# A hybrid decoder block on one core: q, k and v projected channel-major and passed through DRAM

## The chip, the cores and the metric

One core of a Trainium2 chip. The core has four compute engines that run beside each other, each through its own instructions in order: TensorE (PE: matrix products and transposes), VectorE (DVE), ScalarE (ACT) and GpSimd (POOL). SyncE (SP) issues the transfers between DRAM and the on-chip memory (SBUF). Products land in PSUM, which POOL does not read here. The metric is the device time of one execution in microseconds (us); less is better.

## The reference, cut to what matters

All is float32; S = 2048 tokens, 1024 channels, 16 q heads and 4 k/v heads of 64 channels, blocks of 128 tokens.

```python
h = rmsnorm(x, norm_g)
proj = einsum("bsd,de->bse", h, w_in)        # 7680 columns
glu_in, conv_gate, q, k, v, attn_gate, merge_logits = split(proj)
a, b = split(glu_in); c = depthwise_causal_conv(a * sigmoid(b), 31 taps) + bias
c = silu(layernorm(c))
y_conv = (c * silu(conv_gate)) @ w_conv_out
q, k = rope(q), rope(k)      # halves t1, t2 of a head: t1*cos - t2*sin, t2*cos + t1*sin
# each block of 128 queries sees its own block and the one before, window 128, a sink per head
a = softmax_with_sink(q @ k.T / 8) @ v
y_attn = (a * silu(attn_gate)) @ w_attn_out
x = x + (sigmoid(m_c) * y_conv + sigmoid(m_a) * y_attn) @ w_out
return rmsnorm(x)
```

## The kernel before

The tokens go through in two sweeps of 1024, each of two halves of 512. A product in float32 is made as three products of two-part numbers: each operand is split into a rounded part (hi, a cast, mostly on ACT) and the rest (lo, a subtraction), and hi x hi, hi x lo and lo x hi are summed in PSUM.

`project` makes one item: 128 output channels (on partitions) over a sweep, that is 48 matmuls of 128x512, with weights loaded, cast and subtracted by `load_w`. The items of a sweep's first stage are the GLU (gb, ga: `glu_items`) and the gates ag, cg, ma, mc (`gate_item`, eight items each, written to DRAM as d_ag and so on). A GLU item starts one channel block of the convolution: 31 operations on DVE (`conv_ops`, L363 and L367) in a background queue (`line.bg`), issued one per `CONV_EVERY` of TensorE time.

Attention runs in 32 units per sweep (a k/v head g and a token block b: `unit_item`). A unit projects q, k and v of its 128 tokens token-major: 24 matmuls of 128x384 (tile qkv, L463) with weights wqh, wql of that head. Then `attention`, a chain of steps, goes: rope on DVE and POOL (ra, rb), splits into sq, transposes of q and k on TensorE (tq, tk), copies to qT and kT, scores (sc), softmax into ss, transposes of the probabilities (tpp), their split into pt, four selections on POOL that part current and earlier keys (pc, pt), the product with v (ov), and d_att to DRAM. After each step the chain waits for `LAT` us of emitted TensorE time.

```python
LAT = (10.0, 4.0, 15.0, 7.0)   # before tq, sc, tpp, ov
CONV_EVERY = 2.2
```

When all eight convolutions are done, the layer norm starts (`ln_chain`): sums split (csum), the mean by matmuls with ones (lnmu), then eight `ln_center`s on DVE with squares on ACT and the additions of vsum on DVE, then `ln_chain2`: the variance (lnvar), square root, four reciprocals, eight `ln_apply` (cv times rstd on DVE, silu on ACT).

The attention output is then gated: 16 `a_ops` per sweep, each of which loads a gate (lag) and an attention tile (latt) from DRAM through a pool of five buffers (t2k), multiplies them on DVE (L697) and splits the result (aT). `start_tail` releases 14 of them when attention is done and two more when the layer norm is. The items `ya` (attention projection, from aT), `yc` (convolution projection, from uT) and `out_item` follow. At the head of the first ya item stands `line.finish()`, which emits whatever is still waiting.

The order on TensorE is the order of the program text as `Line` emits it; the other engines' orders are set by a scheduler. Between units stand GLU items and gates; after the last unit `start_tail()` comes ahead of the gates that remain.

Of the kernel before, what the change touches and what calls it, by code (L numbers as in the profile page):

```python
# [16 lines left out]
ALU = mybir.AluOpType  # L17
# [18 lines left out]
QKV = GQ * HD + 2 * HD  # L36
# [13 lines left out]
def hybrid_block(ctx: ExitStack, tc: tile.TileContext, x, norm_g, w_in, conv_w, conv_b, ln_g, ln_b,  # L50
                 w_conv, sinks, w_attn, w_out, fin_g, cos_t, sin_t, out):
# [13 lines left out]
    win = w_in[0].rearrange("(k p) e -> p k e", p=P)  # L65
    wconv = w_conv[0].rearrange("(k p) e -> p k e", p=P)
    wattn = w_attn[0].rearrange("(k p) e -> p k e", p=P)
# [26 lines left out]
    def load_first(half):  # L94
        xs = []
        for j in range(4):
            r0 = (4 * half + j) * P
            xs.append(slot(A[8 + 4 * half + j], [P, D], F32, f"xf{half}_{j}"))
            nc.sync.dma_start(out=xs[-1], in_=x2[r0:r0 + P, :])
        return xs  # L100
# [4 lines left out]
    ident_r = const.tile([P, P], F32R, name="ident_r")  # L105
    ident = f(ident_r)
    ident_0 = slot(A[1], [P, P], F32, "ident_0")
    make_identity(nc, ident_0)
    dve.tensor_copy(out=ident_r, in_=ident_0)
    ones_0 = slot(A[2], [P, P], F32, "ones_0")  # L110
# [16 lines left out]
    NR = TAPS + 4  # L127
    rows = slot(A[0], [P, D], F32, "rows")
    nc.sync.dma_start(out=rows[0:TAPS], in_=conv_w[0])
    for i, r in enumerate((norm_g, conv_b, ln_g, ln_b)):  # L130
        nc.sync.dma_start(out=rows[TAPS + i:TAPS + i + 1], in_=r)
    par = const.tile([P, KC, NR], F32, name="par")
    tp = tp_ps.tile([P, 512], F32, tag="tp", name="tp_par")
    for k in range(KC):
        pe.transpose(out=tp[:, k * NR:(k + 1) * NR], in_=rows[0:NR, k * P:(k + 1) * P],
                     identity=ident[0:NR, 0:NR])
    dve.tensor_copy(out=par, in_=tp[:, 0:KC * NR].rearrange("p (k r) -> p k r", r=NR))
# [20 lines left out]
    d_kh = dram.tile([NKV, P, 2 * P], F32, name="d_kh")  # L158
    d_vh = dram.tile([NKV, P, 2 * HD], F32, name="d_vh")

# [1 line left out]
    class Line:  # L162
# [7 lines left out]
        def spend(self, us):  # L170
            """Tensor engine time was emitted: emit what falls due."""
# [3 lines left out]
            while True:  # L175
                if self.bg and self.bg_t <= self.t:
                    self.bg.popleft()()
                    self.bg_t += self.every
                    continue
                if not self.bg:  # L180
                    self.bg_t = max(self.bg_t, self.t)
                due = [c for c in self.late if c[0] <= self.t]
# [15 lines left out]
        def start(self, chain, ok=lambda: True):  # L198
            self.step(chain, ok)

# [30 lines left out]
    def load_w(src, name):  # L231
        """[1024, 128] columns of a matrix as its two float32r parts, by halves of the rows."""
# [11 lines left out]
    def project(src, rhs, name, evac):  # L244
        """128 output columns over the sweep's tokens, channels on partitions: an item for the line."""
# [5 lines left out]
        def blocks():  # L251
            for half in range(2):
# [11 lines left out]
        return prefetch, blocks  # L264
# [13 lines left out]
    def build_h(s, b, tiles):  # L278
        """x block b of sweep s: rmsnorm, transposed, split."""
# [35 lines left out]
    def build_h_first(half, xs):  # L315
        """As build_h, for four blocks at the start of the program."""
# [26 lines left out]
    def sweep(s):  # L343
# [13 lines left out]
        # -- gated linear unit and depthwise convolution --  # L357
# [25 lines left out]
        def glu_items(c):  # L383
# [15 lines left out]
            return [project(win[:, :, C_GLU_B + c * P:C_GLU_B + (c + 1) * P], h_rhs, f"gb{s}_{c}", ev_b),  # L399
                    project(win[:, :, C_GLU_A + c * P:C_GLU_A + (c + 1) * P], h_rhs, f"ga{s}_{c}", ev_a)]  # L400

        # -- gates, kept in DRAM until they are used --
        def gate_item(kind, col, func, e):
# [5 lines left out]
            return project(win[:, :, col + e * P:col + (e + 1) * P], h_rhs, f"{kind}{s}_{e}", ev)  # L409
# [6 lines left out]
        # -- attention --  # L416
        wq, kt, vt = {}, {}, {}

        def load_qkv(g):
            """The weights of a kv head's q, k and v, as eight pieces of work."""  # L420
            tiles, wq[g] = {}, []

            def load(k):
                kp, j = divmod(k, 2)
                if j == 0:
                    tiles["hi"] = slot(AT[2 * kp], [P, 2, QKV], F32R, f"wqh{s}_{g}_{kp}")
                    tiles["lo"] = slot(AT[2 * kp + 1], [P, 2, QKV], F32R, f"wql{s}_{g}_{kp}")
                hi, lo = tiles["hi"][:, j, :], tiles["lo"][:, j, :]
                if s == g == 0:
                    raw = slot(H[8 + k], [P, QKV], F32, f"rawq{s}_{g}_{k}")  # L430
                else:
                    raw = stage.tile([P, QKV], F32, tag="raw", name=f"rawq{s}_{g}_{k}")
                nc.sync.dma_start(out=raw[:, 0:GQ * HD],
                                  in_=win[:, k, C_Q + g * GQ * HD:C_Q + (g + 1) * GQ * HD])
                kv = win[:, k, C_K:C_K + 2 * NKV * HD].rearrange("p (a b) -> p a b", a=2)
                nc.sync.dma_start(out=raw[:, GQ * HD:QKV].rearrange("p (a b) -> p a b", a=2),
                                  in_=kv[:, :, g * HD:(g + 1) * HD])
                act.copy(hi, raw)
                split_lo(lo, raw, hi, pool)
                wq[g].append((hi, lo))  # L440

            return [lambda k=k: load(k) for k in range(KC)]

        done = {}

        def unit_item(g, b):
            got = {}

            def prefetch():
                blk = s * NB + b  # L450
                cs = work.tile([P, 2, HD], F32, tag="cs", name=f"cs{s}_{g}_{b}", bufs=2)
                nc.sync.dma_start(out=cs[:, 0, :], in_=cos_t[blk * P:(blk + 1) * P, :])
                nc.sync.dma_start(out=cs[:, 1, :], in_=sin_t[blk * P:(blk + 1) * P, :])
                got["cs"] = cs

            def blocks():
                ps = mm_ps.tile([P, TH], F32, tag="mm", name=f"qkv{s}_{g}_{b}")
                c0 = (b % 4) * P
                for k in range(KC):
                    hk = hT[b // 4][k]  # L460
                    whi, wlo = wq[g][k]
                    for i, (a, w) in enumerate(((hk[:, 0], whi), (hk[:, 0], wlo), (hk[:, 1], whi))):
                        pe.matmul(out=ps[:, 0:QKV], lhsT=a[:, c0:c0 + P], rhs=w,  # L463
                                  start=(k == 0 and i == 0), stop=(k == KC - 1 and i == 2))
                    if k == KC - 1:
                        n = g * NB + b
                        done[n] = 0
                        line.start(attention(g, b, got["cs"], ps),
                                   lambda: n == 0 or done[n - 1] > min(done[n] + 1, 4))
                    yield 3 * MM_US * QKV / TH  # L470

            return prefetch, blocks

        def attention(g, b, cs, ps):
            u = f"{s}_{g}_{b}"
            n = g * NB + b
            blk = s * NB + b
            cur = b % 2
            first = blk == 0
            nqk = GQ + 1  # L480
            pv = ps[:, 0:nqk * HD].rearrange("p (h d) -> p h d", d=HD)
            ra = t2k(f"ra{u}")[:, 0:nqk * HD].rearrange("p (h d) -> p h d", d=HD)
            rb = t2k(f"rb{u}")[:, 0:nqk * HD].rearrange("p (h d) -> p h d", d=HD)
            hh = HD // 2
            dve.tensor_tensor(out=ra, in0=pv, in1=cs[:, 0:1, :].broadcast_to([P, nqk, HD]), op=ALU.mult)
            pw = pv.rearrange("p h (a d) -> p h a d", d=hh)
            dve.tensor_tensor(out=rb.rearrange("p h (a d) -> p h a d", d=hh), in0=pw[:, :, ::-1, :],  # L487
                              in1=cs[:, 1:2, :].rearrange("p o (a d) -> p o a d", d=hh).broadcast_to(
                                  [P, nqk, 2, hh]), op=ALU.mult)
# [381 lines left out]
```

## Time and profile before

| | before |
|---|---|
| median of three runs | 2251.75 us (2247.3 to 2253.0) |
| span of the profiled execution | 2252.7 us |
| TensorE busy | 2111.2 us (94%) |
| VectorE busy | 1501.2 us (67%) |
| ScalarE busy | 970.0 us (43%) |
| GpSimd busy | 999.7 us (44%) |
| moved by DMA | 205.97 MB, 91 GB/s over the span |

The profile is of one execution, whose own time is its span of 2252.7 us; it lies 1 us above the median of the runs. Lines such as L463 are lines of the kernel file. The groups of instructions list `line engine operation out<-in shapes xcount | busy us, mean ns | idle before it, and what ended the idle time`.

### The profile page before, as it was taken

The page shows a single profiled execution, that of the slowest core. Times are in us where ns is not written, and L with a number is a line of the kernel's source. Part 1 is how long each engine was busy: PE and PEld are TensorE (multiplying, and loading weights), DVE is VectorE, ACT ScalarE, POOL GpSimd, SP SyncE. Part 2 cuts the span into 40 slices and gives each one's busy share as a digit, 9 for nine tenths or more (in the row PEclk, how much of TensorE's full clock was granted, in tenths as well). Part 3 has the DMA queues.
Part 4 walks back from the last instruction along what each step waited for, and adds up shares of the span by engine and source line. Part 5 has one row for each costly group of instructions (what it writes and reads, how often), then busy time and mean ns, then how long its engine had stood idle before and what let it go on. Part 6 is the DMA issues. An engine that isn't in the chain of part 4 may idle for free. (4 is left out here: it accounts for less than half of the span.)

```text
span 2252.7 us, 28431 instructions
## 1 busy us (share of the span) xinstructions
PE 2111.2 (94%) x10000; PEld 1760.6 (78%) x10000; DVE 1501.2 (67%) x2053; ACT 970.0 (43%) x2130; POOL 999.7 (44%) x771
## 2 busy tenths in 40 slices
PE   6998999899899998999999989998998999999998
PEld 6876887787788776888888778777877887878877
DVE  5788787978785746123658878879787858461224
ACT  6454435344535663123454453453444367531212
POOL 3466456446634421242044665565566544222400
PEclk9999999999999999999999999999999999999999
DMA  4122112211312256434331222122113122673331
GB/s 141 50 65 76 60 52 70 69 48 53 95 57 66 90 179 218 120 94 173 113 103 52 62 75 66 48 70 69 52 57 89 53 66 80 209 221 94 99 131 75
DMA packets 255862, 205.97 MB, mean 91 GB/s; under 512 B 48453, under 2 KB 207173, under 8 KB 255720
## 3 DMA queue, kind: packets, MB, share of 16 engines
q1 hardware_dynamic: 255720, 204.16, 29.3%
q8 instruction: 79, 1.29, 0.2%
q14 instruction: 63, 0.52, 0.1%
HBM read 152.98 MB, written 51.12 MB: 91 GB/s over the span
## 5 line engine op out<-in xcount | busy, mean ns | idle before, releaser
L367 DVE SCALAR_TENSOR_TENSOR cv<-glu,par,cv 128x1024 f32<-128x1024 f32 x480 | 730.4, 1522 | 9.3
L463 PE MATMUL qkv<-wqh,hT 128*128 128x384 f32 x1024 | 281.3, 338 | 0.0
L463 PEld LDWEIGHTS qkv<-wqh,hT 128*128 128x128 f32 x1024 | 188.2, 189 | 2.2
L816 PE MATMUL o<-wo,mT 128*128 128x512 f32 x768 | 183.2, 397 | 2.1 <-ACT wo L778 1.9
L559 POOL TENSOR_TENSOR ss<-ss,st 128x512 f32<-128x512 f32 x64 | 98.0, 1532 | 177.0 <-issue 55.2
L495 POOL TENSOR_TENSOR ra<-ra,rb 128x320 f32<-128x320 f32 x64 | 96.3, 1504 | 174.1 <-DVE rb L487 82.3
L463 PE MATMUL qkv<-wql,hT 128*128 128x384 f32 x512 | 172.9, 338 | 0.3 <-POOL wql L229 0.3
L816 PEld LDWEIGHTS o<-wo,mT 128*128 128x128 f32 x768 | 144.3, 189 | 35.0 <-ACT wo L778 2.3
L258 PE MATMUL mm_ya<-aT,whi_ya 128*128 128x512 f32 x512 | 161.7, 397 | 6.4 <-ACT whi_ya L239 3.2
L258 PE MATMUL mm_ag<-hT,whi_ag 128*128 128x512 f32 x512 | 164.1, 402 | 2.1 <-DVE hT L229 2.1
L258 PE MATMUL mm_gb<-hT,whi_gb 128*128 128x512 f32 x512 | 162.6, 399 | 0.9 <-DVE vn L229 0.9
L258 PE MATMUL mm_mc<-hT,whi_mc 128*128 128x512 f32 x512 | 159.9, 394 | 3.3 <-ACT whi_mc L239 3.3
L258 PE MATMUL mm_cg<-hT,whi_cg 128*128 128x512 f32 x512 | 163.0, 400 | 0.0
L258 PE MATMUL mm_ma<-hT,whi_ma 128*128 128x512 f32 x512 | 162.2, 398 | 0.0
L258 PE MATMUL mm_ga<-hT,whi_ga 128*128 128x512 f32 x512 | 159.0, 392 | 1.4 <-ACT glu L389 1.4
L258 PE MATMUL mm_yc<-uT,whi_yc 128*128 128x512 f32 x512 | 158.0, 390 | 0.0
L580 POOL TENSOR_SCALAR_AFFINE_SELECT pt<-pt 128x512 fp32r<-128x512 f32 x120 | 114.8, 956 | 91.7 <-DVE pt L229 85.7
L578 POOL TENSOR_SCALAR_AFFINE_SELECT pc<-pt 128x512 fp32r<-128x512 f32 x120 | 121.5, 1013 | 60.2 <-ACT pt L571 60.1
L555 ACT ACTIVATE ss<-ss,st 128x128 f32<-128x128 f32 x256 | 99.9, 391 | 60.8 <-DVE st L550 60.4
L258 PEld LDWEIGHTS mm_ya<-aT,whi_ya 128*128 128x128 f32 x512 | 97.2, 191 | 29.6 <-ACT whi_ya L239 5.0
L258 PEld LDWEIGHTS mm_mc<-hT,whi_mc 128*128 128x128 f32 x512 | 96.4, 189 | 24.3 <-ACT whi_mc L239 4.2
L258 PEld LDWEIGHTS mm_ag<-hT,whi_ag 128*128 128x128 f32 x512 | 97.2, 193 | 21.9 <-DVE hT L229 3.0
(176 smaller groups left out, 4666.0 us busy)
## 6 DMA issues: line engine op xcount, KB each, us to landing
rawq<-in_w_in_dram SPq DMA_DIRECT2D x64, 128.0 KB, 2.1
raw_gb<-in_w_in_dram SPq DMA_DIRECT2D x32, 256.0 KB, 3.1
raw_ga<-in_w_in_dram SPq DMA_DIRECT2D x32, 256.0 KB, 3.0
raw_ag<-in_w_in_dram SPq DMA_DIRECT2D x32, 256.0 KB, 3.1
d_att<-ss SPq DMA_DIRECT2D x64, 128.0 KB, 1.8
d_ag<-ag SPq DMA_DIRECT2D x32, 256.0 KB, 3.3
raw_cg<-in_w_in_dram SPq DMA_DIRECT2D x32, 256.0 KB, 3.1
d_cg<-cg SPq DMA_DIRECT2D x32, 256.0 KB, 3.4
```

The lines of the kernel that those rows point to most:

```text
L258: pe.matmul(out=ps, lhsT=a, rhs=b, start=(k == 0 and i == 0), stop=(k == KC - 1 and i == 2))
L367: dve.scalar_tensor_tensor(out=cv[c], in0=glu[c][:, j:j + T], scalar=tap(c, j), in1=cv[c], op0=ALU.mult, op1=ALU.add)
L463: pe.matmul(out=ps[:, 0:QKV], lhsT=a[:, c0:c0 + P], rhs=w, start=(k == 0 and i == 0), stop=(k == KC - 1 and i == 2))
L495: pool.tensor_tensor(out=ra, in0=ra, in1=rb, op=ALU.add)
L555: act.activation(out=sb[:, h, :], in_=sb[:, h, :], func=AF.Exp, scale=SCALE, bias=ngm[:, h:h + 1], accum_out=den[:, h:h + 1])
L559: pool.tensor_tensor(out=sb, in0=sb, in1=rinv.unsqueeze(2).broadcast_to([P, GQ, P]), op=ALU.mult)
L578: pool.affine_select(out=pc[:, i], in_=f(pt[:, i]), pattern=[[0, GQ], [1, P]], compare_op=ALU.is_ge, fill=0.0, base=0, channel_multiplier=-1)
L580: pool.affine_select(out=pt[:, i], in_=f(pt[:, i]), pattern=[[0, GQ], [-1, P]], compare_op=ALU.is_gt, fill=0.0, base=0, channel_multiplier=1)
L816: pe.matmul(out=ps, lhsT=a[:, c0:c0 + P], rhs=r, start=(k == 0 and i == 0), stop=(k == KC - 1 and i == 2))
```

## The change

q and k are now items of `project` like the others: 128 channels each, over the whole sweep. The columns of w_in are reordered on the host so that one item holds the first halves of four heads (one q head of each k/v group, or all k heads) and the next the second halves. `rope_items` then rotates between two such items: on evacuation of the first (`ev_a`) DVE multiplies by cos and sin, on evacuation of the second (`ev_b`) likewise, and POOL subtracts and adds. The results are split and written to DRAM (d_q, d_k) with hi and lo. v is an item as well, transposed on TensorE (`v_item`). The twelve items (k, v, q) come first in a sweep.

An attention unit loads its q and k from d_q and d_k by eight DMAs of 32 partitions each (`load_qk`, into three rotating buffers), issued a unit ahead of where its own step begins, and has no projection, rope or transposes of q and k left: scores, softmax, tpp, selections, ov. Units start one per `ATT_EVERY` us of TensorE time, beside the 32 gates, and several buffers of a unit rotate over two or three.

The GLU items are placed by a table, the last ahead of the 38th of 44 other items. `start_tail()` now comes after the last gate item has been handed over; the gates that followed it (`yield from gates`) are gone from there. Weights w_in, w_conv_out and w_attn_out are laid out by the host so that a load takes 2 KB in a row per partition; the parameters of norm and convolution arrive channel-major in one DMA, without tp_par's transposes. At the start, the first GLU and k items run by halves.

```diff
-LAT = (10.0, 4.0, 15.0, 7.0)
-G_EVERY = 3
-G_FIRST = 3
-MM_US = 0.216
+MM_US = 0.2275
+GLU_AFTER = (0, 6, 12, 17, 22, 27, 32, 37)
 CONV_EVERY = 2.2
+ATT_EVERY = 13.4
+LAT = (16.0, 12.0)
...
+        def rope_items(name, e, store):
...
+            def ev_a(half, ps):
+                t = first[half] = slot(AT[4 + half], [P, 2, TH], F32, f"ra{s}_{name}_{half}")
+                dve.tensor_tensor(out=t[:, 0, :], in0=ps, in1=cs[half][:, 0, :], op=ALU.mult)
+                dve.tensor_tensor(out=t[:, 1, :], in0=ps, in1=cs[half][:, 1, :], op=ALU.mult)
+
+            def ev_b(half, ps):
+                a = first[half]
+                b = slot(AT[6], [P, 2, TH], F32, f"rb{s}_{name}_{half}")
+                dve.tensor_tensor(out=b[:, 1, :], in0=ps, in1=cs[half][:, 1, :], op=ALU.mult)
+                dve.tensor_tensor(out=b[:, 0, :], in0=ps, in1=cs[half][:, 0, :], op=ALU.mult)
+                pool.tensor_tensor(out=a[:, 0, :], in0=a[:, 0, :], in1=b[:, 1, :], op=ALU.subtract)
+                pool.tensor_tensor(out=a[:, 1, :], in0=a[:, 1, :], in1=b[:, 0, :], op=ALU.add)
+                for i in range(2):
+                    hl = slot(next_of("hl", AT[7:11]), [P, 2, TH], F32R, f"hl{s}_{name}_{half}_{i}")
+                    put_split(hl, a[:, i, :], dve)
+                    store(i, half, f(hl))
...
-            dve.tensor_tensor(out=ra, in0=pv, in1=cs[:, 0:1, :].broadcast_to([P, nqk, HD]), op=ALU.mult)
...
-            for h in range(GQ):
-                pe.transpose(out=tq[:, h, :], in_=sq[:, h * P:(h + 1) * P], identity=ident_r)
...
+            q, k = qk.pop(n)
+            load_qk(n + 1)
...
+        def start_attention():
+            load_qk(0)
+            for n in range(NKV * NB):
+                line.after(8.0 + n * ATT_EVERY, attention(n))
...
+        for i, item in enumerate(others):
+            if glu_after and i == glu_after[0]:
+                glu_after.pop(0)
+                items = glu_items(KC - 1 - len(glu_after))
+                yield from items
+            if s or i:
+                yield item
+            if i == nqkv:
+                start_attention()
...
         start_tail()
-        yield from gates
         yield ya_item(0, True)
```

How the order moves, first on TensorE at the boundary between the gates and the attention projection in sweep 0. Before (lnvar amid the gate items mc, the last attention units' ov beside it; a digit after a name such as mc_01 is the item and its half):

```order
L590 MATMUL ov_3_6_6716<-pc_3_6_6653,vn_3_6_6248 128x512 x2
L590 MATMUL ov_3_6_6716<-pt_3_6_6650,vn_3_5_6065 128x512 x2
L258 MATMUL mm_mc_01_6697<-hT_1_6_367,whi_mc_01_6508 128x512 x2
L258 MATMUL mm_mc_01_6697<-hT_1_6_367,wlo_mc_01_6509 128x512
L620 MATMUL lnvar_6729<-vsumh_0_6581,ones 128x512
L620 MATMUL lnvar_6729<-vsuml_0_6582,ones 128x512
L620 MATMUL lnvar_6729<-vsumh_1_6585,ones 128x512
L620 MATMUL lnvar_6729<-vsuml_1_6586,ones 128x512
L258 MATMUL mm_mc_01_6697<-hT_1_7_368,whi_mc_01_6508 128x512 x2
L258 MATMUL mm_mc_01_6697<-hT_1_7_368,wlo_mc_01_6509 128x512
L258 MATMUL mm_mc_10_6755<-hT_0_0_135,whi_mc_10_6622 128x512 x2
```

After that row come the rest of eight mc items and then mm_ya. After the change:

```order
L614 MATMUL lnmu_6601<-csuml_1_6504,ones 128x512
L259 MATMUL mm_mc_71_6569<-hT_1_5_313,whi_mc_71_6439 128x512 x2
L259 MATMUL mm_mc_71_6569<-hT_1_5_313,wlo_mc_71_6440 128x512
L259 MATMUL mm_mc_71_6569<-hT_1_6_314,whi_mc_71_6439 128x512 x2
L259 MATMUL mm_mc_71_6569<-hT_1_6_314,wlo_mc_71_6440 128x512
L259 MATMUL mm_mc_71_6569<-hT_1_7_315,whi_mc_71_6439 128x512 x2
L259 MATMUL mm_mc_71_6569<-hT_1_7_315,wlo_mc_71_6440 128x512
L614 MATMUL lnvar_6773<-vsumh_0_6765,ones 128x512
L614 MATMUL lnvar_6773<-vsuml_0_6766,ones 128x512
L614 MATMUL lnvar_6773<-vsumh_1_6769,ones 128x512
L614 MATMUL lnvar_6773<-vsuml_1_6770,ones 128x512
L259 MATMUL mm_ya_00_6816<-aT_0_0_6532,whi_ya_00_6515 128x512 x2
```

The mean and the variance now stand six rows of the last gate item apart, and mm_ya follows the variance at once.

On VectorE, from the sum's split to the centers of the layer norm. Before:

```order
L522 CAST kT_3_5265<-tk_3_6_6358 128x2x128
L625 TENSOR_TENSOR cv_0_758<-cv_0_758,mu_6334 128x1024
L594 TENSOR_TENSOR ss_3_4_6096<-ov_3_4_6340,ss_3_4_6096 64x256
L625 TENSOR_TENSOR cv_1_1486<-cv_1_1486,mu_6334 128x1024
L625 TENSOR_TENSOR cv_2_2169<-cv_2_2169,mu_6334 128x1024
L594 TENSOR_TENSOR ss_3_4_6096<-ov_3_4_6340,ss_3_4_6096 64x256
L635 TENSOR_TENSOR vsum_6337<-vsum_6337,sq_1_0_6365 128x512
L635 TENSOR_TENSOR vsum_6337<-vsum_6337,sq_1_1_6368 128x512
L635 TENSOR_TENSOR vsum_6337<-vsum_6337,sq_2_0_6384 128x512
L635 TENSOR_TENSOR vsum_6337<-vsum_6337,sq_2_1_6387 128x512
L625 TENSOR_TENSOR cv_3_2848<-cv_3_2848,mu_6334 128x1024
L625 TENSOR_TENSOR cv_4_3554<-cv_4_3554,mu_6334 128x1024
```

Centers (L625) and vsum stand between steps of attention units (kT, ss); no lag is near. After:

```order
L230 TENSOR_TENSOR csuml_0_6500<-csum_206,csumh_0_6499 128x512
L230 TENSOR_TENSOR csuml_1_6504<-csum_206,csumh_1_6503 128x512
L619 TENSOR_TENSOR cv_0_511<-cv_0_511,mu_6606 128x1024
L696 TENSOR_TENSOR lag_0_0_6533<-lag_0_0_6533,latt_0_0_6535 128x512
L619 TENSOR_TENSOR cv_1_1135<-cv_1_1135,mu_6606 128x1024
L230 TENSOR_TENSOR aT_0_0_6532<-lag_0_0_6533,aT_0_0_6532 128x512
L696 TENSOR_TENSOR lag_1_0_6550<-lag_1_0_6550,latt_1_0_6552 128x512
L619 TENSOR_TENSOR cv_2_1779<-cv_2_1779,mu_6606 128x1024
L230 TENSOR_TENSOR aT_0_1_6549<-lag_1_0_6550,aT_0_1_6549 128x512
L619 TENSOR_TENSOR cv_3_2588<-cv_3_2588,mu_6606 128x1024
L696 TENSOR_TENSOR lag_2_0_6574<-lag_2_0_6574,latt_2_0_6576 128x512
L619 TENSOR_TENSOR cv_4_3477<-cv_4_3477,mu_6606 128x1024
```

Between the centers (L619) now stand the multiplications lag and splits aT of the gated attention output.

On TensorE, an attention unit's steps among gate matmuls. Before:

```order
L569 MATMUL tpp_0_5_1569<-ident_r,ss_0_5_1358 128x128 x4
L537 MATMUL sc_0_6_1582<-kT_0_458,qT_0_6_1382 128x256 x8
L258 MATMUL mm_ag_21_1555<-hT_1_4_365,whi_ag_21_1408 128x512 x2
L258 MATMUL mm_ag_21_1555<-hT_1_4_365,wlo_ag_21_1409 128x512
L515 MATMUL tq_0_7_1610<-ident_r,sq_0_7_1458 128x128 x4
L518 MATMUL tk_0_7_1615<-ident_r,sq_0_7_1458 128x128 x2
L258 MATMUL mm_ag_21_1555<-hT_1_5_366,whi_ag_21_1408 128x512 x2
L258 MATMUL mm_ag_21_1555<-hT_1_5_366,wlo_ag_21_1409 128x512
```

After (qk is the buffer loaded from d_q and d_k):

```order
L529 MATMUL sc_2_1_4037<-qk_17_3898 128x256 x8
L259 MATMUL mm_cg_60_4011<-hT_0_5_126,whi_cg_61_3877 128x512 x2
L259 MATMUL mm_cg_60_4011<-hT_0_5_126,wlo_cg_61_3878 128x512
L259 MATMUL mm_cg_60_4011<-hT_0_6_127,whi_cg_61_3877 128x512 x2
L259 MATMUL mm_cg_60_4011<-hT_0_6_127,wlo_cg_61_3878 128x512
L259 MATMUL mm_cg_60_4011<-hT_0_7_128,whi_cg_61_3877 128x512 x2
L259 MATMUL mm_cg_60_4011<-hT_0_7_128,wlo_cg_61_3878 128x512
L259 MATMUL mm_cg_61_4075<-hT_1_0_308,whi_cg_60_3871 128x512 x2
L259 MATMUL mm_cg_61_4075<-hT_1_0_308,wlo_cg_60_3872 128x512
L576 MATMUL ov_1_7_4079<-pc_1_7_3963,vt_3_765 128x512 x2
L576 MATMUL ov_1_7_4079<-pt_1_7_3960,vt_3_765 128x512 x2
L556 MATMUL tpp_2_0_4090<-ident_r,ss_2_0_3916 128x128 x4
```

The transposes tq and tk are gone, and scores are read from the loaded tile.

More of the change, by code (lines that the diff above doesn't have):

```diff
@@ L126, in hybrid_block @@
     dve.tensor_scalar(out=nsink, in0=sink_bc, scalar1=-1.0, scalar2=None, op0=ALU.mult)
[L127 to L131, printed above, removed]
-    par = const.tile([P, KC, NR], F32, name="par")
[L133 to L137, printed above, removed]
+    par = const.tile([P, KC, NR], F32, name="par")
+    nc.sync.dma_start(out=par, in_=par_d)
     def tap(c, j):
@@ L251, in blocks @@
         def blocks():
-            for half in range(2):
+            for half in halves:
                 ps = mm_ps.tile([P, TH], F32, tag="mm", name=f"mm_{name}{half}")
@@ L414, in load_gate @@
             return g
[L417 to L472, printed above, removed]
@@ L474, in attention, with load_rope @@
-        def attention(g, b, cs, ps):
+        cs = {}
+        def load_rope():
+            for half in range(2):
+                cs[half] = slot(AT[11 + half], [P, 2, TH], F32, f"cs{s}_{half}")
+                t0 = s * T + half * TH
+                nc.sync.dma_start(out=cs[half], in_=rope_t[:, :, t0:t0 + TH])
+        def rope_items(name, e, store):
+            first = {}
+            def ev_a(half, ps):
[13 more added lines that the diff above has]
+                    store(i, half, f(hl))
+            return [project(w_in[e], h_rhs, f"{name}a{s}", ev_a),
+                    project(w_in[e + 1], h_rhs, f"{name}b{s}", ev_b)]
@@ new lines, in store_k, with store_q, store @@
+        def store_k(i, half, hl):
+            t0 = s * T + half * TH
+            nc.sync.dma_start(out=d_k[:, i, :, t0:t0 + TH].rearrange("a p t -> p a t"), in_=hl)
+        def store_q(r):
+            def store(i, half, hl):
+                b0 = s * NB + 4 * half
+                for a in range(2):
+                    nc.sync.dma_start(out=d_q[a, i, :, b0:b0 + 4, r, :],
+                                      in_=hl[:, a, :].rearrange("p (b t) -> p b t", t=P))
+            return store
+        vt = {}
@@ L486, in attention @@
[L486 to L489, printed above, removed]
-            v = work.tile([P, 2, HD], F32R, tag="vn", name=f"vn{u}", bufs=4)
-            vt[(g, b)] = v
-            vps = ps[:, nqk * HD:QKV]
-            act.copy(v[:, 0, :], vps)
```

225 lines of the change are left out of this document (127 added, 98 removed).

## The prediction

> **What bounds the kernel now.** I read the page first, for who is busy. Columns: busy us (share of the span) and number of instructions; then tenths of forty slices.
>
> ```profile
> PE 2111.2 (94%) x10000; PEld 1760.6 (78%) x10000; DVE 1501.2 (67%) x2053; ACT 970.0 (43%) x2130; POOL 999.7 (44%) x771
> ...
> DVE  5788787978785746123658878879787858461224
> ```
>
> TensorE (PE) is the bound, at 94% of 2252.7 us. VectorE (DVE) averages 67%, but the slices show two plateaus of 7 to 9 tenths (the gates and attention of each sweep) and two valleys. So there are two questions: how many microseconds of TensorE work the change saves, and where TensorE waits. The table of waits has the second (who waits, for whom; total us, times, longest us):
>
> ```profile
> PE ov L590 <- POOL pc L578: 30.4, 20, 5.6
> PE sc L537 <- DVE kT L522: 20.1, 17, 2.7
> PE tq L515 <- DVE st L558: 16.5, 15, 2.0
> PE ov L590 <- POOL pt L580: 16.3, 20, 2.1
> PE tp_par L135 <- DMA rows<-in_conv_ln_b_dram: 15.1, 1, 15.1
> PE tpp L569 <- POOL ss L559: 3.7, 3, 1.6
> ...
> PE mm_ya L258 <- ACT whi_ya L239: 3.2, 3, 1.3
> PE mm_ya L258 <- POOL wlo_ya L229: 2.9, 4, 0.9
> PE mm_ya L258 <- ACT aT L267: 2.9, 1, 2.9
> ...
> PE tq L515 <- DVE sq L229: 2.1, 2, 1.1
> PE ov L590 <- DVE pt L229: 2.1, 2, 1.3
> ```
>
> Of some 141 us of idle TensorE (2252.7 - 2111.2), the attention rows (ov, sc, tq, tpp) hold 91.2 us in 79 waits, the start 15.1, the first attention projection (mm_ya) 9.0. A matmul is drawn longer than the pace at which its successors start, so a row understates its wait. The chain of waits gives the paces (start us, us, what, how many):
>
> ```profile
> 1826.58 3.67 PE qkv L463 x21
> ...
> 2012.65 53.33 PE mm_ya L258 x226
> 2065.97 76.95 PE mm_yc L258 x339
> ```
>
> A 128x512 matmul starts every 76.95/339 = 0.227 us, a 128x384 one every 3.67/21 = 0.175. An undisturbed 128x512 matmul is drawn 0.39 long (groups below), so each wait is about 0.17 longer than its row: 79 x 0.17 = 13, and attention waits cost about 104 us.
>
> **The change part by part.**
>
> *q, k, v by 128x512 instead of 128x384.* The groups:
>
> ```profile
> L463 PE MATMUL qkv<-wqh,hT 128*128 128x384 f32 x1024 | 281.3, 338 | 0.0
> L463 PE MATMUL qkv<-wql,hT 128*128 128x384 f32 x512 | 172.9, 338 | 0.3 <-POOL wql L229 0.3
> ...
> L258 PE MATMUL mm_yc<-uT,whi_yc 128*128 128x512 f32 x512 | 158.0, 390 | 0.0
> ```
>
> 1536 x 0.175 = 268.5 us go. What comes is 12 items of 48 matmuls in each of two sweeps: 1152 x 0.227 = 261.5. **-7.**
>
> *Transposes of q and k.* The timeline at one unit (start, us, what):
>
> ```profile
> 1272.29 0.45 PE L515 MATMUL tq<-ident_r,sq 128*128 128x128 f32 x4
> 1272.57 0.33 PE L518 MATMUL tk<-ident_r,sq 128*128 128x128 f32 x2
> 1272.74 0.41 PE L463 MATMUL qkv<-wqh,hT 128*128 128x384 f32 x1
> ```
>
> Six transposes take 0.45 us; 64 units, 28.8. The v transposes that come (32 of them, at 0.075) take 2.4. **-26.**
>
> *Attention waits.* tq and the copy kT are gone: their 38.7 us of rows cannot return there. Scores now read a tile loaded from DRAM and issued a unit ahead, 13.4 us; a 256 KB load lands in 3.9 (latt, below), so I cost that at nothing. If SyncE's queue, which also issues the weights and stores and waits for their buffers in order, held these loads up by 9 us or more, the scores would wait instead. The ov waits (48.8 in rows) are the selects on POOL being late; the gap between tpp and ov grows from 7 us to 12 of TensorE time, and the longest wait is 5.6, so they should nearly vanish. tpp, 15 before and 16 now, keeps its waits. The units do run closer together than before, one in 13.4 us, so not everything goes: I leave 20 of the 104. Bounds: 0 and all 104 left. **-84.**
>
> *Rope.* Per q or k half, DVE has four multiplications and two splits where it had ra, rb and two splits per unit, about the same elements, but earlier: before attention. POOL loses the 64 additions of ra and gets two per half. All lies beside matmuls; its cover is a half item (24 x 0.227 = 5.4 us) per PSUM buffer, three buffers. The stores to d_q, d_k and the reloads add DMA in a stage that leaves room (DMA share is the number ahead of GB/s; PEclk ahead of it):
>
> ```profile
> 100.00:700.00 600.00, 553.11 (x2696) 463.96 (x2695) 499.40 (x616) 264.61 (x611) 337.95 (x247) 0.98 0.22 64
> 1150.00:1850.00 700.00, 655.01 (x3230) 555.97 (x3229) 545.29 (x705) 310.76 (x722) 389.39 (x287) 0.98 0.22 64
> 732.00:776.00 44.00, 42.41 (x206) 34.80 (x205) 32.55 (x52) 30.02 (x68) 21.35 (x17) 1.00 0.27 83
> ```
>
> 0. The granted clock of 0.98 over these 1300 us is 26 us lost; with most waits gone I take back 10 (bounds 0 and 26). **-10.** Parameters by one DMA instead of rows and transposes (tp_par): the first matmuls still need x loaded, so of 15.1 I take **-2** (bounds -8, +5). Host-tiled weights: 0, since the weight waits in the table above (whi_ya, wlo_ya) come to 6.1 us and stand on the casts and splits, not on the loads.
>
> *The boundary between gates and attention projection.* This is the term that decides. Before, the layer norm's statistics, its application and the 16 gate multiplications of attention (a_ops: load gate, load att, multiply, split) run beside gate matmuls: the third window above, from the mean (lnmu) to the variance (lnvar), has TensorE busy 42.41 of 44 us. The starts of the two, and what a_ops cost (least, median, greatest ns; first and last start):
>
> ```profile
> L620 PE MATMUL lnmu<-csumh,ones x4: 389/393/397, 732.5 to 1854.6; 128*128 128x512 f32 x4
> L620 PE MATMUL lnvar<-vsumh,ones x4: 389/395/397, 773.1 to 1894.9; 128*128 128x512 f32 x4
> L697 DVE TENSOR_TENSOR lag<-lag,latt x16: 677/693/1803, 1936.3 to 1982.8; 128x512 f32<-128x512 f32 x16
> DMA to landing us min/median/max: 3.1/3.3/4.1
> latt<-d_att SPq DMA_DIRECT2D x32, 256.0 KB, 3.9
> ```
>
> After it, the last GLU item stands seven items (7 x 48 x 0.227 = 76 us) before the end of the gates, and its 31 conv operations are issued one in 2.2 us (68 us). So lnmu comes nine matmuls before the last gate ends; the a_ops are released only then; and lnvar stands ahead of mm_ya in TensorE's order. Everything between is bare. On DVE:
>
> ```profile
> L642 DVE TENSOR_TENSOR cv<-cv,rstd 128x1024 f32<-128x1024 f32 x16 | 24.2, 1584 | 0.0
> L229 DVE TENSOR_TENSOR aT<-lag,aT 128x512 fp32r<-128x512 f32 x32 | 22.7, 711 | 20.4 <-ACT aT L267 20.2
> L635 DVE TENSOR_TENSOR vsum<-vsum,sq 128x512 f32<-128x512 f32 x28 | 21.4, 813 | 1.3 <-ACT sq L634 1.1
> L625 DVE TENSOR_TENSOR cv<-cv,mu 128x1024 f32<-128x1024 f32 x16 | 21.4, 1367 | 0.1
> L639 DVE RECIPROCAL rstd<-rstd 128x256 f32<-128x256 f32 x8 | 13.6, 1728 | 6.5 <-ACT rstd L661 6.5
> L661 ACT ACTIVATE rstd<-lnvar,eps_t 128x1024 f32<-128x1024 f32 x2 | 2.2, 1116 | 0.0
> ```
>
> lnmu to lnvar holds 8 centers (8 x 1.37 = 10.9), 14 a_ops (14 x (0.69 + 0.71) = 19.6), 14 additions of vsum (14 x 0.81 = 11.4), two splits (1.4): 43 us of DVE, and about 4 ahead of it for the mean's matmuls and copy. The a_ops' 28 loads go through five buffers; before, one a_op came every (1982.8 - 1936.3)/15 = 3.1 us with gates sharing the buffers, which for 14 alone would be at most 43 us, beside the centers. I take 50, less the nine matmuls (2.0): 48 bare. Then the square root with its table (2.4), four reciprocals (6.9), a multiplication, eight applications (12.7) and five short operations stand before the last aT that mm_ya's second half needs: 27 us against 42 matmuls of cover (9.5): 17 more; 15 with some operations at their shortest. A window over the a_ops of before shows what waits do to the clock: PEclk 0.97 of 60 us.
>
> ```profile
> 1930.00:1990.00 60.00, 55.29 (x230) 43.75 (x230) 31.19 (x38) 24.14 (x39) 14.16 (x11) 0.97 0.78 250
> ```
>
> That is 1.8 us; 2 per sweep. So 65 per sweep, 130 for both, less the present mm_ya waits of 9.0: **+121.** Bounds: +80 (DVE's operations at their shortest, loads free) and +150 (loads at 3.1 per a_op, not overlapped with the centers). [...]
>
> *Sum against this execution:* 2252.7 - 7 - 26 - 84 - 10 - 2 + 121 = 2244.7; with the median of the runs 1 us under the span, **2243**. Two large terms of opposite sign nearly cancel.
>
> **The rivals.**
>
> *Slower: attention's waits stay, moved to tpp and ov.* DVE runs conv operations between the softmax steps, and conv is slower when POOL works too (least, median, greatest ns):
>
> ```profile
> L367 DVE SCALAR_TENSOR_TENSOR cv<-glu,par,cv x480: 1245/1285/2406, 75.8 to 1809.4; 128x1024 f32<-128x1024 f32 x160
> L367 DVE SCALAR_TENSOR_TENSOR cv<-glu,par,cv 128x1024 f32<-128x1024 f32 x480 | 730.4, 1522 | 9.3
> ```
>
> The mean of 1522 lies 237 above the median: some take 2.4 us. With a unit per 13.4 us, POOL's normalisation and four selects and DVE's steps meet conv denser than now. For it: DVE was busy 499.4 of 600 us there, and waits of 104 us did occur. Against it: rope is gone from the units. It decides from 0.25 us more per unit (64 x 0.25 = 16, past 2258); at 0.9 us, half the old wait, it gives 2243 + 58 = 2301. Chance 0.24. [...]
>
> *Slower, smaller: rope holds PSUM.* In the twelve q, k, v items DVE has about six operations per half beside conv; if it lags by more than the cover, a microsecond for each of 40 halves gives 2283. Conv operations are short and interleaved, so 0.06.
>
> *Faster: the boundary is short and attention's waits all go.* a_ops' loads run ahead, DVE at its shortest: +80 instead of +121, and 0 of the 104 left: 2243 - 41 - 20 = 2182; half of it, 2212. Chance 0.17 for under 2212.
>
> *The boundary costs nothing,* as gates cover it: the order on TensorE rules it out.
>
> **How the numbers follow.** Forecast 0.53, its own range 2212 to 2265. No change here means within 0.3% of 2251.75, 2245 to 2258.5, about what a measurement can tell. Of the forecast's 0.53, 0.29 lies under 2245, 0.15 in the band, 0.09 above; the faster rival gives 0.17 faster, the slower two 0.01 in the band, 0.29 above. Faster 0.46, same 0.16, slower 0.38. The range reaches half into the rivals on both sides: 2195 to 2302.
>
> **What would show it.** Right: no tq, tk; ov and sc among the waits with under 20 us; between lnmu and lnvar, twice, a TensorE idle of about 48 us with DVE full, and a second of about 15 in mm_ya's first item, released by aT. Wrong: if TensorE idles under 80 us at the two boundaries together, or if tpp and ov wait over 60 us, or a new row (sc on a qk load, a PSUM wait in the rope items) is over 15.

## The result, and the profile after

The changed kernel takes 2330.4 us (median of four runs, 2326.9 to 2334.6) against 2249.5 before (median of four runs, 2247.0 to 2253.0): a ratio of 1.036 (95% interval 1.034 to 1.038). It is slower, where 2243 was forecast, and lies 28 us above the range.

The page of the changed kernel, busy times and slices:

```profile
PE 2095.6 (90%) x9256; PEld 1697.2 (73%) x9256; DVE 1474.7 (63%) x1804; ACT 907.4 (39%) x1913; POOL 949.2 (41%) x738
...
PE   7998999989999946999999989989899899279998
DVE  3968749585885758223676869577685955671224
```

TensorE is busy 15.6 us less than before (2111.2), and the span is 2327.8, so its idle time rose from 141.5 to 232.2 us. Two holes stand in its slices, one per sweep (4 and 6, then 2 and 7 tenths), where DVE shows 5 and 8, then 6 and 7. The table of waits (who, for whom; us, times, longest) says who holds it up:

```profile
PE lnvar L614 <- ACT vsumh L604: 86.1, 2, 44.3
PE mm_ya L259 <- ACT aT L271: 24.0, 2, 12.7
PE mm_cg L259 <- POOL wlo_cg L230: 22.0, 10, 4.5
PE mm_ag L259 <- POOL wlo_ag L230: 17.0, 6, 5.2
PE mm_ma L259 <- POOL wlo_ma L230: 14.7, 6, 5.3
PE mm_q_a L259 <- ACT whi_q_a L240: 11.2, 2, 5.6
...
PE tpf L336 <- DVE ident_r L114: 8.4, 1, 8.4
PE mm_mc L259 <- POOL wlo_mc L230: 7.9, 3, 3.8
PE mm_gb L259 <- ACT whi_gb L240: 7.2, 3, 5.5
PE tpp L556 <- POOL ss L551: 5.8, 7, 3.0
```

Sums over all rows of this table, before and after, in us:

| TensorE waits | before | after |
|---|---|---|
| attention (tq, sc, tpp, ov) | 93.3 | 5.8 |
| boundary (lnvar; mm_ya for aT) | 3.1 | 110.6 |
| weights (whi, wlo, and wql before) | 13.8 | 86.7 |

Attention's waits went, further than forecast, the boundary opened as forecast, and a third group came that the forecast had at 0: waits for weights. Before, the largest row of that group, beside the two of mm_ya in the prediction's table, was

```profile
PE mm_mc L258 <- ACT whi_mc L239: 3.3, 2, 3.1
```

The prediction's own sign of being wrong, a new row over 15 us, is there twice (wlo_cg and wlo_ag), though it named a qk load and a PSUM wait as examples and not weights. The boundary in the timeline of TensorE, sweep 0 (start, us, what; in brackets the idle time and who ended it):

```profile
838.16 0.40 PE L259 MATMUL mm_mc<-hT,wlo_mc 128*128 128x512 f32 x1
880.35 0.79 PE L614 MATMUL lnvar<-vsumh,ones 128*128 128x512 f32 x1 [41.80 <-ACT vsumh L604]
```

and the same stretch by engine (PE busy 2.20 of 44 us, DVE 37.62; PEclk 0.53):

```profile
838.00:882.00 44.00, 2.20 (x6) 1.22 (x5) 37.62 (x52) 20.62 (x36) 1.65 (x1) 0.53 0.57 183
```

DVE is what bounds this hole, with centers, a_ops and vsum as the order had them. Half of its 37.62 us there belongs to the a_ops; this is the same stretch for the tile lag alone (DVE busy 18.66 us: 14 multiplications and 14 subtractions of aT):

```profile
838.00:882.00 44.00, 18.66 (x28) 8.63 (x14) 0.53 0.57 183
```

The first matmuls behind the hole are drawn 0.79 us instead of 0.39, and the granted clock was 0.50 until 884, 0.66 in the next 2 us and 1.00 from 886:

```profile
882.00:884.00 2.00, 2.00 (x6) 1.52 (x6) 0.00 (x0) 1.32 (x2) 0.00 (x0) 0.50 0.83 226
884.00:886.00 2.00, 2.00 (x8) 1.59 (x7) 0.91 (x2) 0.00 (x0) 0.00 (x0) 0.66 0.74 242
886.00:888.00 2.00, 2.00 (x11) 1.63 (x10) 2.00 (x2) 0.00 (x0) 0.00 (x0) 1.00 0.90 305
```

From the first matmul at 880.35 that is some 5 us below the full clock, which cost 2 to 3 us a hole (an estimate from these clocks: half of the 3.65 us to 884 and a third of the next 2).

A wait for weights, in the queue of GpSimd (POOL) in sweep 1:

```profile
1441.03 1.56 POOL L567 TENSOR_SCALAR_AFFINE_SELECT pt<-pt 128x512 fp32r<-128x512 f32 x1 [4.32 <-DVE pt L230]
1442.55 1.61 POOL L565 TENSOR_SCALAR_AFFINE_SELECT pc<-pt 128x512 fp32r<-128x512 f32 x1
1444.23 0.64 POOL L567 TENSOR_SCALAR_AFFINE_SELECT pt<-pt 128x512 fp32r<-128x512 f32 x1
1445.00 1.92 POOL L551 TENSOR_TENSOR ss<-ss,st 128x512 f32<-128x512 f32 x1
1446.88 2.34 POOL L377 TENSOR_TENSOR csum<-csum,cv 128x1024 f32<-128x1024 f32 x1
1449.18 1.25 POOL L230 TENSOR_TENSOR wlo_ag<-raw_ag,whi_ag 128x512 fp32r<-128x512 f32 x1
```

and on TensorE at the same time:

```profile
1450.49 0.80 PE L259 MATMUL mm_ag<-hT,wlo_ag 128*128 128x512 f32 x1 [5.20 <-POOL wlo_ag L230]
```

The subtraction that makes wlo_ag takes 1.25 us. It stands behind a selection that waited 4.32 us for DVE's pt, two more selections, a normalisation and a sum of the convolution. Two theories follow: a *queue* theory (casts and subtractions are late because ScalarE and GpSimd stand behind attention steps that wait for VectorE) and a *buffer* theory (with three buffers, the next item's second half of weights can be made only from the last 2.7 us (12 matmuls at 0.227) of the present item on, and must be there 2.7 us into the next, so that a delay soon hits TensorE). And for the boundary, that its 110 us are separate from these and return if it is undone.

### The profile page after: what moved, and what is told of

Read it like the earlier page. It is cut to its first block, busy times and chain, and to the rows that moved or that the text cites. A ratio compares the mean times of both kernels' runs of the same rounds, so it can differ in the third digit from the quotient of the medians.

```text
span 2327.8 us, 26914 instructions
## 1 busy us (share of the span) xinstructions
PE 2095.6 (90%) x9256; PEld 1697.2 (73%) x9256; DVE 1474.7 (63%) x1804; ACT 907.4 (39%) x1913; POOL 949.2 (41%) x738
## 5 line engine op out<-in xcount | busy, mean ns | idle before, releaser
L371 DVE SCALAR_TENSOR_TENSOR cv<-glu,par,cv 128x1024 f32<-128x1024 f32 x480 | 744.8, 1552 | 10.0
L567 POOL TENSOR_SCALAR_AFFINE_SELECT pt<-pt 128x512 fp32r<-128x512 f32 x120 | 126.8, 1060 | 98.0 <-DVE pt L230 56.2
L230 POOL TENSOR_TENSOR wlo_ya<-raw_ya,whi_ya 128x512 fp32r<-128x512 f32 x32 | 44.3, 1385 | 256.0 <-ACT whi_ya L240 248.6
L565 POOL TENSOR_SCALAR_AFFINE_SELECT pc<-pt 128x512 fp32r<-128x512 f32 x120 | 115.1, 961 | 72.4 <-ACT pt L558 59.8
L551 POOL TENSOR_TENSOR ss<-ss,st 128x512 f32<-128x512 f32 x64 | 92.0, 1438 | 127.7 <-DVE st L550 62.0
L537 DVE COPY_PREDICATED ss<-causal,sc 128x512 f32<-128x512 int32 x64 | 47.2, 738 | 129.9 <-ACT ss L536 123.7
L259 PE MATMUL mm_cg<-hT,wlo_cg 128*128 128x512 f32 x256 | 103.5, 404 | 22.1 <-POOL wlo_cg L230 22.0
L259 PE MATMUL mm_ag<-hT,wlo_ag 128*128 128x512 f32 x256 | 102.9, 402 | 17.0 <-POOL wlo_ag L230 17.0
L259 PE MATMUL mm_ma<-hT,wlo_ma 128*128 128x512 f32 x256 | 104.0, 406 | 14.7 <-POOL wlo_ma L230 14.7
L259 PEld LDWEIGHTS mm_gb<-hT,whi_gb 128*128 128x128 f32 x512 | 96.1, 191 | 28.7 <-ACT whi_gb L240 8.3
```

The source lines that it names most:

```text
L230: eng.tensor_tensor(out=out_, in0=full, in1=f(hi), op=ALU.subtract)
L259: pe.matmul(out=ps, lhsT=a, rhs=b, start=(k == 0 and i == 0), stop=(k == KC - 1 and i == 2))
L371: dve.scalar_tensor_tensor(out=cv[c], in0=glu[c][:, j:j + T], scalar=tap(c, j), in1=cv[c], op0=ALU.mult, op1=ALU.add)
L537: dve.copy_predicated(out=sb, mask=causal_i, data=sc[:, :, 1, :])
L551: pool.tensor_tensor(out=sb, in0=sb, in1=rinv.unsqueeze(2).broadcast_to([P, GQ, P]), op=ALU.mult)
L565: pool.affine_select(out=pc[:, i], in_=f(pt[:, i]), pattern=[[0, GQ], [1, P]], compare_op=ALU.is_ge, fill=0.0, base=0, channel_multiplier=-1)
```

## The experiments

**e1: the boundary undone.**

```diff
-GLU_AFTER = (0, 6, 12, 17, 22, 27, 32, 37)
+GLU_AFTER = (0, 5, 10, 14, 18, 22, 26, 30)
...
+            if i == len(others) - KC - 1:
+                start_tail()
...
-        start_tail()
         yield ya_item(0, True)
```

> The changed kernel with its boundary undone: the GLU items earlier (0, 5, 10, 14, 18, 22, 26, 30), so that the convolution ends some 100 us before the gates do, and start_tail ahead of the last eight gates, as before the change. Boundary theory: lnvar's wait for vsumh (86.1 us in the changed kernel's profile) and mm_ya's for aT (24.0) go, with the cold clock behind them a few us more, and the attention stage keeps its waits for weights: 2330 - 110 to 120 = 2210 to 2220. Rival: VectorE's work is only moved into the gates' stage, where it is already full for stretches of 50 us, so that half or more comes back there as waits for weights: 2265 or more.

2259.8 us (2258.0 to 2266.8), ratio to before 1.005 (1.003 to 1.006): 70 us faster than the changed kernel. The rows of lnvar and aT are gone, which took 107 us of waits away, yet the time fell by 37 less. The largest rows that are left:

```profile
PE mm_gb L259 <- POOL wlo_gb L230: 23.0, 9, 4.8
PE mm_cg L259 <- POOL wlo_cg L230: 17.2, 8, 3.5
PE tpp L556 <- POOL ss L551: 12.6, 11, 3.0
PE mm_mc L259 <- ACT mc L410: 12.0, 2, 6.2
...
PE sc L529 <- DMA d_ag<-ag: 7.9, 1, 7.9
PE sc L529 <- DMA qk<-d_k: 7.5, 1, 7.5
```

Weights cost 90.7 us in rows, 4.0 more than in the changed kernel, and have moved: gb, in the GLU items, which had 9.1 with whi and wlo together, now has 30.3, and the gates have less. What came back stands in other rows: sc 15.4 (the first unit of each sweep, for its loads), mm_mc 12.0 (for ScalarE's evacuation of mc), tpp 6.8 more. So the boundary theory is shown for the place and for two thirds of the size. The rival had the size nearly right (2265; the time lies just under it) but not the rows, since it expected the loss as waits for weights. The forecast of 2210 to 2220 was too good. The waits of sc were a term that the prediction had named and costed at nothing (loads held up in SyncE's queue). In the order of e1 no GLU items stand any more between the last q items and the first unit; that this is their cause is argued here; e8 starts the unit later.

**e2: half the taps.**

```diff
-CONV_EVERY = 2.2
+CONV_EVERY = 4.4
...
-            for j in range(1, TAPS):
+            for j in range(2, TAPS, 2):
```

> The changed kernel without 15 of the 31 taps of each convolution (the output is not the reference's), the others issued half as often (CONV_EVERY 4.4), so that the convolution ends and the layer norm starts at the same place. Queue theory: the weights' casts (ScalarE) and subtractions (GpSimd) stand in those engines' queues behind attention steps that wait for VectorE; with VectorE relieved, TensorE's waits for whi and wlo in the q, v and gate items (about 90 us) fall under 30 and the time to about 2260, the boundary's 110 us staying. Rival: the weights are late because the third of three buffers is freed too late for any delay, or because SyncE's queue brings them late: they stay over 60 us, and the time over 2300.

One run, 2235.9 us, some 94 us under the changed kernel and 24 under what was expected. Weights fell from 86.7 to 33.9 in rows (5.4 of both at the start of the program); attention has 1.4, the boundary its 109.4. The largest row of weights that is left:

```profile
PE mm_ma L259 <- POOL wlo_ma L230: 9.4, 4, 3.4
```

The rest of the gain is that TensorE is busy 2064.8 us instead of 2095.6, with the same matmuls. Granted clock and TensorE's busy time in the attention stage, changed kernel and then this one:

```profile
250.00:700.00 450.00, 425.26 (x1956) 346.42 (x1955) 336.10 (x411) 244.05 (x546) 254.32 (x201) 0.97 0.34 104
```

```profile
250.00:700.00 450.00, 439.97 (x2070) 363.20 (x2070) 234.24 (x366) 265.56 (x595) 232.06 (x219) 0.99 0.36 110
```

DVE is busy 234 us there instead of 336, and 2070 matmuls run instead of 1956. So VectorE's convolution makes most of the delays. The run does not say by which way: GpSimd waits less for VectorE's steps (its selections of pt wait 25.6 us for DVE's pt, against 56.2), and its own operations are shorter too (232.06 us for 219 of them, against 254.32 for 201). The 33.9 us lie just over the 30 that I named; from a single run, that is no finding.

**e3: a fourth buffer for weights.**

```diff
-    stage = ctx.enter_context(tc.tile_pool(name="stage", bufs=3))
+    stage = ctx.enter_context(tc.tile_pool(name="stage", bufs=4))
```

> The changed kernel with four instead of three buffers each for the raw, hi and lo halves of weights, so that both halves of the next item can be loaded, cast and subtracted while the present one is used. Buffer theory: with three, the next item's second half can be cast only when the present item has used its first half, 2.7 us before its end, and must be there 2.7 us into the next; in the kernel before, an attention unit's projection stood in between as cover. Waits for weights fall from about 90 to 35 us or less: 2265 to 2285. Queue theory: the casts and subtractions stay where they stand in the queues of ScalarE and GpSimd, and the waits stay: 2315 to 2335.

2274.9 us (2274.0 to 2275.9), ratio to before 1.011 (1.009 to 1.012): 55 us faster than the changed kernel, in the buffer theory's range and far from the queue theory's. Its table of waits:

```profile
PE lnvar L614 <- ACT vsumh L604: 86.0, 2, 43.9
PE tpp L556 <- POOL ss L551: 43.4, 19, 4.4
...
PE mm_gb L259 <- ACT whi_gb L240: 5.5, 1, 5.5
```

Of 86.7 us of weight waits 5.5 are left, one at the start. DVE is busy 1471.8 us and POOL 948.6, against 1474.7 and 949.2, so only the lead of the weights was changed (of their loads, casts and subtractions together). What POOL's delay still does shows next in line: tpp waits 43.4 us for the normalisation, against 5.8. So both theories hold a part: VectorE's load makes most of the delay (e2), and three buffers let it through to TensorE as a wait for weights (e3).

**e4: the kernel before, with start_tail late.**

```diff
-        start_tail()
         yield from gates
+        start_tail()
```

> The kernel before with one edit: start_tail() behind the last eight gate items instead of ahead of them, so that only the 16 a_ops of each sweep (not the layer norm) lose their cover. Boundary theory: 16 a_ops at 2.4 to 3.1 us stand bare ahead of or within mm_ya's first item (11 us of matmuls): 30 to 38 us a sweep, 2310 to 2325. Rival: their loads are ready in the queue by then and VectorE does one in 1.4 us, so most is hidden: under 2275.

2283.2 us (2281.9 to 2284.9), ratio 1.014 (1.012 to 1.016): 32 us lost, between the two expectations, 16 us a sweep instead of 30 to 38. The largest new row:

```profile
PE mm_ya L258 <- ACT aT L267: 17.5, 15, 2.4
```

and the a_ops of sweep 1 (first and last start):

```profile
L697 DVE TENSOR_TENSOR lag<-lag,latt x16: 683/686/1787, 1976.6 to 2014.8; 128x512 f32<-128x512 f32 x16
```

Where nothing else uses the five buffers, an a_op comes every (2014.8 - 1976.6)/15 = 2.5 us instead of 3.1 beside gates, and mm_ya's own matmuls run between them. So the a_ops without the layer norm cost 32 of the boundary's 110 us. How the rest divides was not run: in the changed kernel both stand in one hole, where the a_ops hold half of DVE's busy time (18.66 of 37.62 us, above).

**e5: e1 and e3 together.** The edits of both.

> The boundary's repair (earlier GLU items, start_tail ahead of the last eight gates) and the fourth weight buffer together. If the two costs are separate, as the theory has it, the gains add: 2330 - 70 - 55 = 2205, and what wlo waits came back with the boundary's repair (57 us in rows) go too, so down to 2190. Rival: both relieve the same queue, and VectorE, full earlier, brings tpp's wait for the normalisation to 60 us or more: 2225 to 2245.

2212.3 us (2209.2 to 2216.1), ratio 0.984 (0.982 to 0.986). The gains nearly add: 70 + 55 = 125 were expected off 2330, and 118 came; the time lies 7 us over the expected 2190 to 2205 and under the rival's 2225. Weights cost 5.5 us in rows, the boundary 5.3. Of the weight waits that e1 left (90.7) only 47 us turned into time, since the delay came out at tpp:

```profile
PE tpp L556 <- POOL ss L551: 47.0, 23, 4.1
```

**e6: other addresses.**

```diff
-    v_halo = const.tile([P, NKV, 2, HD], F32R, name="v_halo")
+    v_halo = work.tile([P, NKV, 2, HD], F32R, tag="v_halo", name="v_halo", bufs=1)
```

> The changed kernel with one edit that changes no instruction's work: the tile v_halo (2 KB per partition) is kept behind the weight buffers instead of ahead of everything else, so that all tiles of activations and weights lie at the addresses they had before the change, 2 KB lower. In the traces the pace of 128x512 matmuls went from 0.227 to 0.230 us in the gates and yc, with the same instructions. Address theory: the pace goes back to 0.227 and the time falls by about 8900 x 0.0025 = 20 us, to 2308. Rival: the pace comes from the denser traffic of transfers or from the engines beside: 2325 to 2335.

2330.8 us (2330.3 to 2333.9), ratio 1.037 (1.036 to 1.039): no change, and mm_yc kept a pace of 0.230 us (78.03/339, where the kernel before had 76.95/339 = 0.227):

```profile
2144.69 78.03 PE mm_yc L259 x339
```

Tiles lie 2 KB lower in this kernel, though not each where it lay before the change, since the slots are taken in another order. So this shift by 2 KB is ruled out as the cause; addresses altogether are not. The rival's causes, denser traffic and the engines beside, do not fit the yc items either (windows in the last section).

**e7: all edits, and tpp at 18 us.** e1, e3 and e6, with LAT = (18.0, 12.0).

> Everything together: the boundary's repair, the fourth weight buffer, v_halo moved, and tpp issued 18 us instead of 16 after the scores, since with four buffers tpp waits 43 us for the normalisation. If the costs are separate: 2190 to 2205 less 20 for the pace and less about 15 of tpp's waits: 2160 to 2180. Rival: the pace stays and tpp's waits move to ov: 2200 or more.

2206.5 us (2200.7 to 2213.0), ratio 0.983 (0.980 to 0.985). The interval overlaps e5's, and the expected 2160 to 2180 was missed: tpp's waits fell to 8.2 and ov's rose to 30, as the rival had it, and the pace stayed.

```profile
PE ov L576 <- POOL pc L565: 21.1, 10, 5.0
...
PE ov L576 <- POOL pt L567: 9.0, 9, 2.7
...
PE sc L529 <- DMA d_ag<-ag: 8.4, 1, 8.4
PE tpp L556 <- POOL ss L551: 8.2, 6, 1.9
```

**e8: e7 with the first unit later.** LAT = (17.0, 13.0), and units from 20 us instead of 8.

> The kernel with everything together (e7), and the first attention unit of a sweep 20 instead of 8 us after the q items (its scores waited 8.4 and 8.1 us for their loads in e7's profile), with tpp 17 us after the scores and ov 13 after that (18 and 12 in e7, where ov waited 30 us for the selections and tpp 8). If these waits have no other cause: 2206 - 16 - 10 = 2180, 2175 to 2195. Rival: the units end later, and the gated attention output comes late at mm_ya: 2205 or more.

2222.5 us (2217.4 to 2224.9), ratio 0.986 (0.984 to 0.989): not the 2175 to 2195 expected, and if anything slower than e7, whose interval (0.980 to 0.985) its own just touches. The two waits of sc for loads (8.4 and 8.1 us in e7) went, so they did hang on the early start. But tpp is back, and mm_ya waits for aT, since the units end later (the last a_op of sweep 1 starts at 1957.8 us, in e7 at 1935.8):

```profile
PE tpp L556 <- POOL ss L551: 48.5, 23, 4.7
PE mm_ya L259 <- ACT aT L271: 12.1, 9, 3.0
```

Which of the edits cost what stays open. In e7 and e8 such delays moved the wait rather than removed it. The best version is e7, or e5, which differs from it by less than the runs spread; both are some 1.7% faster than the kernel before.

## Why the prediction was wrong, step by step

*The step that failed* is one clause, "Host-tiled weights: 0", with the reason that weight waits stood at 6.1 us in the rows quoted. That reads a wait's size in the old order. Before, a unit's projection (24 matmuls of 128x384, 4.2 us, and no weights of load_w) and its transposes mostly stood between one gate item and the next, and covered the making of the second half's weights; the change took them out, and I priced their removal only as work saved. What it cost: 86.7 us of waits in place of 13.8, shown to hang on the buffers by e3.

That it was the projection that covered them, the two traces bear out. In the kernel before, the same delay in GpSimd's queue cost nothing:

```profile
1377.56 1.55 POOL L580 TENSOR_SCALAR_AFFINE_SELECT pt<-pt 128x512 fp32r<-128x512 f32 x1 [1.81 <-DVE pt L229]
...
1382.23 2.25 POOL L229 TENSOR_TENSOR wlo_ag<-raw_ag,whi_ag 128x512 fp32r<-128x512 f32 x1
```

and on TensorE:

```profile
1386.59 0.34 PE L463 MATMUL qkv<-wqh,hT 128*128 128x384 f32 x1
...
1389.95 0.39 PE L258 MATMUL mm_ag<-hT,wlo_ag 128*128 128x512 f32 x1
```

The subtraction ends at 1384.48, some 8 us after its buffer came free (the old weights' last matmul starts at 1376.25), and TensorE needs it at 1389.95: from 1379.74 to 1386.77 it had a projection to do, with steps of other units in it. Taken over the GLU and gate items of both traces, but for the first of the program: the second half's subtraction ended more than 6.8 us after its buffer came free in 27 of 95 items before and in 29 of 94 after, so the delay did not grow. But from the buffer's release to the time when TensorE could use the weights there were 10.9 us before (median) and 6.8 after. The subtraction was too late for TensorE in 7 items before, in none of the 57 with a projection in that stretch, and in 30 after. No run put the projection back alone.

*Attention, -84:* right in number (the rows fell from 93.3 to 5.8), in part by luck. The slower rival had the delays right (POOL's normalisation and selections behind VectorE) and their exit wrong: they came out at wlo, not at tpp and ov. With that exit closed (e3), tpp waits 43.4 us and ov 2.7, where 20 were left for attention; that is the rival, at half its size. Its row of conv operations, parted by what POOL did in the trace of before: with no POOL operation beside them they took 1.28 us in the mean (145 operations, none over 1.29), with one 1.63 (335).

*The boundary, +121:* right in kind, a little large. lnvar waited 43 us a sweep where 48 were taken, aT 12 where 17 were; 110.6 less the 9.0 of before is +102, with 2 to 3 us a sweep of lower clock, by the estimate above. I took the a_ops at 3.1 us each, the pace of a stage that shares their buffers; e4 has them at 2.5 us.

*Work, -33:* the transposes and qkv went, but TensorE's busy time fell by 15.6 only. Two things took the rest. The first is the waits for weights, behind which a matmul is drawn longer (0.80 us at 1450.49, in place of 0.39): in e3 the same matmuls, without these waits (though with those of tpp), are busy 2075.6 us, 20 less. The second is the pace. The chain of the changed kernel has for the last yc items (before: 0.227)

```profile
2143.09 85.86 PE mm_yc L259 x372
```

That is 0.231 us, 1.7% more for the same instructions; e3 has it too (88.59 us for 384), so it does not come from the waits. Over the 5376 matmuls of GLU, gates and yc it would be some 15 us (an estimate, with 0.0025 to 0.0035 us each). Its cause stays open; e6 rules out its shift by 2 KB.

*Clock, -10:* wrong in sign. The granted clock in the attention stage fell from 0.98 to 0.97 (0.96 in sweep 1), where I had taken some of the loss back; in e2, with 33.9 us of weight waits in place of 86.7, it was 0.99. Behind the wait of 5.20 us that ended at 1450.49 the granted clock (third number from the end) is 0.50:

```profile
1452.00:1454.00 2.00, 2.00 (x6) 1.59 (x6) 0.92 (x3) 0.71 (x2) 1.60 (x3) 0.50 0.84 263
```

*Start, -2:* the wait for rows (15.1) became one of 8.4 for the identity and 5.5 for the first weights: right. (The 5.5 are among the 86.7 of weights.)

In sum, idle time by rows: -87.5 (attention) + 101.5 (boundary) + 79 (weights, without mm_ya's, which are in the boundary's 9.0) - 2 (the rest) = +91, and -15.6 of work: +75, the difference of the two spans. Without the weights' 79 the sum would have been near the forecast of -8, but only as arithmetic, and with luck: work, clock and start came out 27 us worse than their -45, the boundary some 20 better. Nor do the 79 come off alone: e3 takes them away and runs 2274.9, since tpp then waits.

## What to carry to other kernels

When a change takes work off the bounding engine, ask what was being made ready behind that work: here 4.2 us of projection between two gate items hid the casts and subtractions of the next weights, and with it gone, delays that GpSimd had before as well reached TensorE as waits of up to 5.3 us. Where one engine holds both a chain's steps and the supply of the bounding engine, as GpSimd did here, the chain's delays can reach the supply (a wait of 4.32 us for pt on GpSimd, then one of 5.20 us for wlo_ag on TensorE); one more buffer for the supply (55 us here for a changed number) is the first thing to try. Then look where the delay comes out next: here at tpp, with 43.4 us. And a layer norm that ends with the gates stood bare here for 43 us a sweep, so a paced background must end early enough for what follows it.

## What the runs showed of the hardware

The 128x512 matmuls of mm_yc, which wait for nothing, started every 0.227 us in the kernel before and its variant e4 (76.95 and 77.04 us for 339 in the chain), and every 0.230 to 0.231 in the changed kernel and its variants, on three chips (88.57 to 88.59 us for 384 in e3, e5, e7 and e8), with the same instructions. Windows of 76 us at a granted clock of 1.00 show what it is not: first the kernel before, in mm_yc and in the output items o,

```profile
2066.00:2142.00 76.00, 76.00 (x335) 62.68 (x335) 20.29 (x29) 17.14 (x29) 34.59 (x27) 1.00 0.33 97
2168.00:2244.00 76.00, 76.00 (x331) 61.99 (x330) 25.83 (x43) 18.01 (x44) 0.00 (x0) 1.00 0.10 42
```

then the changed kernel, in the same two:

```profile
2146.00:2222.00 76.00, 76.00 (x331) 61.96 (x330) 20.23 (x29) 16.71 (x28) 33.83 (x27) 1.00 0.29 93
2242.00:2318.00 76.00, 76.00 (x331) 61.91 (x331) 24.61 (x43) 18.00 (x44) 0.00 (x0) 1.00 0.13 49
```

The items o run at the slower pace (331 in 76 us) in both kernels, so it does not belong to a whole kernel; and in mm_yc the changed kernel moves no more data (93 GB/s against 97) and has the other engines as busy, so traffic and neighbours do not explain it. What sets the pace was not found.
